# Attention outputs computed channel-major, with normalised probabilities, in a hybrid RWKV-7 and sliding-window attention layer

## The chip, the core and the metric

The kernel runs on one core of a Trainium2 chip. The metric is the time on the device in microseconds (us) of one execution; smaller is better. TensorE (PE, its weight loads PEld) multiplies matrices into the PSUM banks, VectorE (DVE), ScalarE (ACT) and GpSimd (POOL) work elementwise, and SyncE (SP) and ScalarE issue DMA transfers. Each engine runs its instructions in the order in which the program lists them, and waits for the others by semaphores.

## The reference

One decoder layer for 1,024 tokens and 2,048 channels. An RMS norm feeds one input projection (6,528 columns), whose columns go to two groups of heads: RWKV-7 time mixing (16 heads of 64) and sliding-window attention (16 query heads of 64, 2 key/value heads, window 128, blocks of 128 queries). Gated outputs of both are joined, projected and added to the input. The change is in the attention:

```python
logits = einsum('bnqhgd,bnkhd->bnhgqk', qb, kb) * HEAD_DIM ** -0.5   # kb: previous and own block
logits = where(mask, logits + bias, -inf)
m = maximum(max(logits, -1), sink)
e = exp(logits - m)
p = e / (sum(e, -1) + exp(sink - m))
o = einsum('bnhgqk,bnkhd->bnqhgd', p, vb)
return o * silu(g)
```

## The kernel before

The tokens are taken in two halves of 512 (4 blocks of 128). For each half, `hprep` makes the transposed input, and then 8 units follow, one per pair of heads of each kind. A unit has six "z tiles": each is 48 main matmuls of 128x512 into one of two `z` banks (L346 and L347 by turns, then four of L351, for each of four quarters of the contraction). Of a unit's six, three feed the RWKV part (`rwkv_prep`, `rwkv_chain`, `rwkv_post`), one its gate, and two the attention `att` (queries and gate). After both halves the output projection (L786 to L788) runs. Main matmuls take float32 operands split into two float32r parts; the small matmuls of the attention and of RWKV are plain float32.

The order on each engine is made when the program is built. Every step carries a due time (the numbers behind `yield`, set by `at`), in a planner's microseconds: a main matmul counts 0.32, a z tile 15.36, a unit 92.16. Among the instructions that can go, the one with the smallest due time goes first. Matmuls of the z tiles so fill what the small steps leave. `att` counts from the start of its own unit, and `rwkv` too. The attention of a unit is due 99 to 143 after the unit's start, so most of it lies in the next unit, 92.16 later: its output matmuls (due +133) at 40.84 of the next unit, in the third z tile (which starts at 30.72), beside that unit's `rwkv_prep` (due +0.3 to +59). In `rwkv_prep` the chain is: L390 and L391 (matmuls, due +18.5) into `m` banks; L393 to L405 (activations and a scan, L399); L554 and L555 (a sum over heads, in `headsum`); L409 to L427 (VectorE makes Gt and F); L437 (matmuls of Gt and F, due +55 and +59).

Tiles of one name (tag) share a fixed number of buffers: three PSUM banks for `m`, five SBUF buffers of 128x512 for `ta`.

In `att` one unit handles two heads. For each, scores are made (L682 to L690), biased (L695), reduced to a maximum, exponentiated on ScalarE with the row sums (L704), and VectorE takes the reciprocals `sm` of the sums with the sink's part (L705, L706). The unnormalised probabilities of the four blocks are transposed on TensorE (L711) and split by the mask into the part for the own block's keys `pc` (L714) and the previous one's `pv` (L715). The output matmuls (L723 for `pc`, L725 for `pv`) have the probabilities as weights (128x128) and 64 columns of values as the moving side; they give query-major outputs. VectorE multiplies by `sm` (L730, one instruction per head), TensorE transposes the result (L734), and VectorE multiplies with the gate (L736). ScalarE issues the DMA of the result (L737).

Of the kernel before, what the change touches and what calls it, by code (L numbers as in the profile page):

```python
# [14 lines left out]
ALU = mybir.AluOpType  # L15
# [4 lines left out]
P = 128  # L20
# [8 lines left out]
NB = T // P  # L29
# [35 lines left out]
def layer(tc, x, norm_w, w_in, w_out, mu_rwkv, w0, w2, a0, a2, k_k, k_a, r_k, lnx_w, lnx_b,  # L65
# [7 lines left out]
    V, A, G, PE = nc.vector, nc.scalar, nc.gpsimd, nc.tensor  # L73

    def sb(shape, tag, bufs=1, dt=F32):
        return pool.tile(list(shape), dt, name=tag, tag=tag, bufs=bufs)

    HR = (slice(0, 64), slice(64, 128))
    NT = dict(t=4, ta=5, zt=5, wr=4, wh=3, wl=3)

    def tmp(tag="t"):
        return sb([P, T], tag, NT.get(tag, 1))

    def ps(tag, shape=(P, 512)):
        return psum.tile(list(shape), F32, name=tag, tag=tag, bufs={"z": 2, "m": 3, "o": 1, "ch": 1}[tag])
# [6 lines left out]
    def at(t):  # L92
        tc.cur_priority = 100000 + int(t * 1000)
# [24 lines left out]
    ident, causal, mT, ind2 = cs[:, 0:128], cs[:, 128:256], cs[:, 256:384], cs[:, 384:386]  # L118
# [92 lines left out]
    vt = sb([P, NB + 1, P], "vt")  # L211
# [23 lines left out]
    def rsqrt(v, n, tag):  # L235

        y = sb([P, n], tag + "y", 2)
        a = sb([P, n], tag + "a", 2)
        V.tensor_scalar(y[:].bitcast(I32), v.bitcast(I32), -0.5, MAGIC, ALU.mult, ALU.add)
        for _ in range(3):  # L240
            V.tensor_tensor(a[:], y[:], y[:], ALU.mult)
            V.scalar_tensor_tensor(a[:], v, -0.5, a[:], ALU.mult, ALU.mult)
            V.scalar_tensor_tensor(y[:], a[:], 1.5, y[:], ALU.add, ALU.mult)
        return y
# [312 lines left out]
    def silu2(g):  # L557

        tg = tmp("ta")
        A.activation(tg[:], g, AF.Tanh, scale=0.5)  # L560
        s = sb([P, T], "sil", 2)
        V.scalar_tensor_tensor(s[:], tg[:], 1.0, g, ALU.add, ALU.mult)
        return s
# [95 lines left out]
    def att(t0, hf, p, Q, sq, gz):  # L659
        yield t0 + 99  # L660
        sil = silu2(gz[:])
        yield t0 + 103
        pq = ps("m")
        for b in range(NB):
            PE.matmul(pq[:, b * 2:b * 2 + 2], lhsT=sq[:, b * P:(b + 1) * P], rhs=ind2, start=True, stop=True)
        ms = sb([P, 8], "qms", 2)
        V.tensor_scalar(ms[:], pq[:, 0:8], 1.0 / 64, 1e-6, ALU.mult, ALU.add)
        rq = rsqrt(ms[:], 8, "q")
        bia = sb([P, 2, P], "bia")
        nc.sync.dma_start(bia[:], bass.AP(tensor=bd.tensor, offset=bd[p:p + 1, 0:1].offset, ap=[[P - 1, P], [8 * P * P, 2], [1, P]]))  # L670
        yield t0 + 108.5
        pts, sms = [], []
        Ls = [tmp("ta")[:].rearrange("p (b k) -> p b k", b=NB) for _ in range(2)]
        for b2 in range(2):
            yield t0 + 103.5 + 4 * b2
            pls = [ps("m", (P, 2, 256)) for _ in range(2)]
            for b in range(2):
                lb = b2 * 2 + b
                ks = 1 if hf * NB + lb == 0 else 0
                qs, kc = slice(lb * P, (lb + 1) * P), slice((lb + ks) * P, (lb + 2) * P)  # L680
                for i, pl in enumerate(pls):
                    PE.matmul(pl[:, b, ks * P:256], lhsT=Q[:, i, qs], rhs=kh[i][:, kc], start=True, stop=False)  # L682
                    PE.matmul(pl[:, b, ks * P:256], lhsT=Q[:, i, qs], rhs=kl[i][:, kc], start=False, stop=True)
            for pl, L3 in zip(pls, Ls):
                if hf == 0 and b2 == 0:
                    V.memset(L3[:, 0, :], NEG)
                    A.copy(L3[:, 1, :], pl[:, 1, 0:128])
                else:
                    A.copy(L3[:, b2 * 2:b2 * 2 + 2, :], pl[:, :, 0:128])
                V.copy_predicated(L3[:, b2 * 2:b2 * 2 + 2, :], causal_i[:, None, :].to_broadcast([P, 2, P]), pl[:, :, 128:256])  # L690
        for i, L3 in enumerate(Ls):
            hd = p + 8 * i
            yield t0 + 105 + 7 * i
            for b in range(NB):
                V.scalar_tensor_tensor(L3[:, b, :], L3[:, b, :], rq[:, b * 2 + i:b * 2 + i + 1], bia[:, i, :], ALU.mult, ALU.add)  # L695
            mx = sb([P, NB], "mx", 2)
            V.tensor_reduce(mx[:], L3, axis=AX.X, op=ALU.max)
            nm = sb([P, NB], "nm", 2)
            V.tensor_scalar(nm[:], mx[:], snk[:, hd:hd + 1], -1.0, ALU.max, ALU.mult)
            es = sb([P, NB], "es", 2)  # L700
            A.activation(es[:], nm[:], AF.Exp, bias=snk[:, hd:hd + 1])
            sm = sb([P, NB], "sm", 4)
            for b in range(NB):
                A.activation(L3[:, b, :], L3[:, b, :], AF.Exp, bias=nm[:, b:b + 1], accum_out=sm[:, b:b + 1])  # L704
            V.tensor_tensor(sm[:], sm[:], es[:], ALU.add)  # L705
            V.reciprocal(sm[:], sm[:])  # L706
            sms.append(sm)
            yield t0 + 125 + 2 * i
            pt = ps("m", (P, NB, P))
            for b in range(NB):  # L710
                PE.transpose(pt[:, b, :], L3[:, b, :], ident)  # L711
            pc, pv = tmp("ta"), tmp("ta")
            r3 = lambda t: t[:].rearrange("p (b k) -> p b k", b=NB)
            V.tensor_tensor(r3(pc), pt[:], mT[:, None, :].to_broadcast([P, NB, P]), ALU.mult)  # L714
            V.tensor_tensor(r3(pv), pt[:], r3(pc), ALU.subtract)  # L715
            pts.append((r3(pc), r3(pv)))

        yield t0 + 133
        po = ps("m", (P, NB, 2, 64))
        for b in range(NB):  # L720
            blk = hf * NB + b
            for i in range(2):
                PE.matmul(po[:, b, i, :], lhsT=pts[i][0][:, b, :], rhs=vt[:, b + 1, i * 64:(i + 1) * 64], start=b == 0 and i == 0, stop=False, skip_group_check=True)  # L723
                if blk > 0:
                    PE.matmul(po[:, b, i, :], lhsT=pts[i][1][:, b, :], rhs=vt[:, b, i * 64:(i + 1) * 64], start=False, stop=b == NB - 1 and i == 1, skip_group_check=True)  # L725
        ot = tmp("ta")
        o4 = ot[:].rearrange("p (b i v) -> p b i v", b=NB, i=2)
        at(t0 + 125)
        for i in range(2):
            V.tensor_tensor(o4[:, :, i, :], po[:, :, i, :], sms[i][:, :, None].to_broadcast([P, NB, 64]), ALU.mult)  # L730
        yield t0 + 143
        po = ps("m")
        for b in range(NB):
            PE.transpose(po[:, b * P:(b + 1) * P], ot[:, b * P:(b + 1) * P], ident)  # L734
        y = tmp("ta")
        V.scalar_tensor_tensor(y[:], po[:], 0.5, sil[:], ALU.mult, ALU.mult)  # L736
        nc.scalar.dma_start(yd[hf, NP + p], y[:])  # L737
# [146 lines left out]
```

## Time and profile before

| | |
|---|---|
| median of 3 runs | 2084.99 us (2084.62 to 2093.28) |
| profiled execution | 2082.83 us |
| its span, first to last instruction | 2081.0 us |
| mean granted TensorE clock | 0.989 |

The span is the time between the first and the last instruction of the profiled execution; what lies around it, 1.8 us, is not seen in the trace. An engine's busy time says how long it had an instruction in work; TensorE's matmuls are pipelined, so the duration of one (some 400 ns for a main matmul) is longer than the distance to the next (some 235 ns). The distances are what counts on TensorE.

### The profile page before, as it was taken

To read this page: it belongs to the slowest core of one execution; us is meant where nothing else is said; L and a number is where in the kernel's file an instruction comes from. 1 tells how busy PE (TensorE), PEld (TensorE's weight loads), DVE (VectorE), ACT (ScalarE), POOL (GpSimd) and SP (SyncE) were. 2 spreads that over 40 slices of the span, in tenths; PEclk is the share of its full clock that TensorE was granted. 3 is DMA by queue.
4 is the path that set the end of the run, shared out by engine and by line. 5 is a ranking of instruction groups with operands and counts; after the bars stand their busy time and mean duration, and the time that the engine had idled before them with its cause. 6 is when DMAs were issued, how large, how long until landed. Compare 5 with 4: busy or idle time off the path is not lost. (4 is left out here: it accounts for less than half of the span.)

```text
span 2081.0 us, 36561 instructions
## 1 busy us (share of the span) xinstructions
PE 1990.9 (96%) x13216; PEld 1638.3 (79%) x13216; DVE 1158.1 (56%) x2680; ACT 1034.9 (50%) x2563; POOL 862.9 (41%) x740
## 2 busy tenths in 40 slices
PE   7999999999999998998999999999999989999999
PEld 5777778787878786776878787877778778988887
DVE  5647575748475765756565666757575763011001
ACT  5455556465656464735546464555546463223221
POOL 4643444434353433244443534343443433444443
PEclk9999999999999999999999999999999989999999
DMA  7332323332332325123232323232323353555443
GB/s 179 94 85 69 82 72 87 76 81 70 81 86 70 91 60 150 57 77 73 72 83 62 94 57 95 61 92 66 80 72 86 75 166 116 154 156 170 135 137 117
DMA packets 412293, 197.02 MB, mean 95 GB/s; under 512 B 216941, under 2 KB 381136, under 8 KB 412112
## 3 DMA queue, kind: packets, MB, share of 16 engines
q1 hardware_dynamic: 371360, 181.90, 31.9%
q10 hardware_dynamic: 40000, 11.67, 2.3%
q0 software_dynamic: 752, 1.11, 0.5%
q8 instruction: 104, 1.70, 0.3%
q14 instruction: 77, 0.63, 0.1%
HBM read 173.51 MB, written 21.10 MB: 94 GB/s over the span
## 5 line engine op out<-in xcount | busy, mean ns | idle before, releaser
L322 POOL TENSOR_TENSOR wl<-wr,wh 128x512 fp32r<-128x512 f32 x536 | 711.2, 1331 | 1095.3 <-ACT wh L321 497.9
L346 PE MATMUL z<-hh,wh 128*128 128x512 f32 x1632 | 669.2, 410 | 8.7 <-ACT ta L650 6.6
L347 PE MATMUL z<-hl,wh 128*128 128x512 f32 x1632 | 651.1, 399 | 0.6 <-DVE hl L263 0.6
L321 ACT CAST wh<-wr 128x512 fp32r<-128x512 f32 x536 | 329.6, 618 | 465.3 <-PE z L347 158.1
L351 PE MATMUL z<-hh,wl 128*128 128x512 f32 x1632 | 468.8, 402 | 0.3 <-POOL wl L322 0.3
L346 PEld LDWEIGHTS z<-hh,wh 128*128 128x128 f32 x1632 | 309.0, 189 | 77.1 <-ACT ta L650 7.0
L347 PEld LDWEIGHTS z<-hl,wh 128*128 128x128 f32 x1632 | 309.2, 189 | 58.7 <-DVE hl L263 1.2
L351 PEld LDWEIGHTS z<-hh,wl 128*128 128x128 f32 x1632 | 297.7, 189 | 60.4 <-POOL wl L322 1.0
L353 DVE TENSOR_TENSOR z<-z,R 128x512 f32<-128x512 f32 x102 | 70.9, 695 | 137.4 <-PE z L351 134.5
L786 PE MATMUL z<-wh,hh 128*128 128x256 f32 (+1 forms) x352 | 113.1, 322 | 4.1 <-DVE ta L794 4.1
L588 DVE SCALAR_TENSOR_TENSOR svu<-ch,pe,s 64x64 f32<-64x64 f32 x224 | 63.3, 282 | 95.8 <-PE ch L584 91.8
L788 PE MATMUL z<-wh,hl 128*128 128x256 f32 (+1 forms) x352 | 112.3, 319 | 0.0
L787 PE MATMUL z<-wl,hh 128*128 128x256 f32 (+1 forms) x352 | 112.0, 318 | 0.0
L580 ACT ACTIVATE s<-svu,pe 64x64 f32<-64x64 f32 x256 | 88.2, 344 | 39.1 <-DVE svu L588 35.3
L577 PEld LDWEIGHTS o<-svu,F 128*128 128x128 f32 x512 | 78.2, 189 | 16.2 <-DVE svu L588 4.6
L794 DVE TENSOR_TENSOR ta<-z,ta 128x256 f32<-128x256 f32 (+1 forms) x22 | 10.0, 491 | 126.6 <-PE z L788 126.1
L437 PE MATMUL m<-F,Gt 64*128 64x128 f32 x512 | 52.8, 296 | 28.1 <-DVE F L427 14.3
L577 PE MATMUL o<-svu,F 128*128 128x64 f32 x512 | 77.6, 265 | 1.9 <-ACT svu L535 1.3
L437 PEld LDWEIGHTS m<-F,Gt 64*128 64x128 f32 x512 | 42.3, 193 | 44.3 <-issue 26.7
L794 DVE TENSOR_TENSOR ta<-m,ta 128x512 f32<-128x512 f32 x9 | 6.1, 690 | 124.8 <-PE m L788 124.8
L786 PEld LDWEIGHTS z<-wh,hh 128*128 128x128 f32 x352 | 68.0, 193 | 9.0 <-DVE ta L794 3.4
L787 PEld LDWEIGHTS z<-wl,hh 128*128 128x128 f32 x352 | 68.1, 194 | 4.3
(278 smaller groups left out, 3388.9 us busy)
## 6 DMA issues: line engine op xcount, KB each, us to landing
wr<-in_w_in SPq DMA_DIRECT2D x280, 256.0 KB, 2.9
wr<-in_w_in SPq DMA_DIRECT2D x256, 128.0 KB, 2.5
wr<-in_w_out SPq DMA_DIRECT2D x64, 256.0 KB, 3.0
wr<-in_w_out SPq DMA_DIRECT2D x128, 128.0 KB, 2.9
ta<-in_x SPq DMA_DIRECT2D x37, 256.0 KB, 5.2
zt<-yd SPq DMA_DIRECT2D x32, 256.0 KB, 3.3
out<-ta SPq DMA_DIRECT2D x24, 256.0 KB, 3.9
yd<-ta ACTq DMA_DIRECT2D x16, 256.0 KB, 2.0
```

The source lines that it names most:

```text
L321: A.copy(hi[:], raw)
L322: G.tensor_tensor(lo[:], raw, hi[:].bitcast(F32), ALU.subtract)
L346: PE.matmul(z[:], lhsT=wh, rhs=hh[kk][:], start=(kk == 0), stop=False)
L347: PE.matmul(z[:], lhsT=wh, rhs=hl[kk][:], start=False, stop=False)
L351: PE.matmul(z[:], lhsT=lo[:, k * P:(k + 1) * P], rhs=hh[kk][:], start=False, stop=(kk == KT - 1))
L353: V.tensor_tensor(z[:], z[:], R[:], ALU.mult)
L437: PE.matmul(b[:, c, :], lhsT=Gt[hr, c0 + c, :], rhs=F[c0 // 4][hr, i, c, :], start=True, stop=True)
L577: PE.matmul(O[:, c, i, :], lhsT=F[c // 4][:, i, c % 4, :], rhs=svu[:, i, c, :], start=c % 4 == 0 and i == 0, stop=False, skip_group_check= ...
L580: A.activation(s0[hr], svu[hr, i, c, :], AF.Copy, scale=pe[hr, c:c + 1])
L786: PE.matmul(o, lhsT=yh[k][:, ts], rhs=wh, start=k == 0 and tt % n == 0, stop=False, skip_group_check=True)
L787: PE.matmul(o, lhsT=yh[k][:, ts], rhs=wl, start=False, stop=False, skip_group_check=True)
L788: PE.matmul(o, lhsT=yl[k][:, ts], rhs=wh, start=False, stop=k == KT - 1 and tt % n == n - 1, skip_group_check=True)
```

## The change

The reciprocal `sm` of the sums is applied ahead of the transposes: four scalings of 128x128 per head on VectorE (eight per unit). The transposes are due 2 later. The output matmuls have operands swapped: 64 columns of values are the weights, 128 columns of probabilities the moving side, and the outputs come channel-major, one head in each half of the output partitions (`HR`). They are due at +137, not +133. The two multiplications behind them and the transposes of the outputs go, and the gate multiplication reads the outputs' bank directly.

```diff
-        pts, sms = [], []
+        pts = []
...
             V.reciprocal(sm[:], sm[:])
-            sms.append(sm)
-            yield t0 + 125 + 2 * i
+            for b in range(NB):
+                V.tensor_scalar(L3[:, b, :], L3[:, b, :], sm[:, b:b + 1], None, ALU.mult)
+            yield t0 + 127 + 2 * i
             pt = ps("m", (P, NB, P))
             for b in range(NB):
                 PE.transpose(pt[:, b, :], L3[:, b, :], ident)
...
-
-        yield t0 + 133
-        po = ps("m", (P, NB, 2, 64))
+        yield t0 + 137
+        po = ps("m")
         for b in range(NB):
             blk = hf * NB + b
-            for i in range(2):
-                PE.matmul(po[:, b, i, :], lhsT=pts[i][0][:, b, :], rhs=vt[:, b + 1, i * 64:(i + 1) * 64], start=b == 0 and i == 0, stop=False, skip_group_check=True)
+            ts = slice(b * P, (b + 1) * P)
+            for i, hr in enumerate(HR):
+                PE.matmul(po[hr, ts], lhsT=vt[:, b + 1, i * 64:(i + 1) * 64], rhs=pts[i][0][:, b, :], start=b == 0, stop=False, skip_group_check=True)
+            for i, hr in enumerate(HR):
                 if blk > 0:
-                    PE.matmul(po[:, b, i, :], lhsT=pts[i][1][:, b, :], rhs=vt[:, b, i * 64:(i + 1) * 64], start=False, stop=b == NB - 1 and i == 1, skip_group_check=True)
-        ot = tmp("ta")
-        o4 = ot[:].rearrange("p (b i v) -> p b i v", b=NB, i=2)
-        at(t0 + 125)
-        for i in range(2):
-            V.tensor_tensor(o4[:, :, i, :], po[:, :, i, :], sms[i][:, :, None].to_broadcast([P, NB, 64]), ALU.mult)
-        yield t0 + 143
-        po = ps("m")
-        for b in range(NB):
-            PE.transpose(po[:, b * P:(b + 1) * P], ot[:, b * P:(b + 1) * P], ident)
+                    PE.matmul(po[hr, ts], lhsT=vt[:, b, i * 64:(i + 1) * 64], rhs=pts[i][1][:, b, :], start=False, stop=b == NB - 1, skip_group_check=True)
         y = tmp("ta")
         V.scalar_tensor_tensor(y[:], po[:], 0.5, sil[:], ALU.mult, ALU.mult)
```

## Rows read from the trace of the kernel before

**Rows 1.** The page, part 1: busy time, share of the span, instructions.
```profile
PE 1990.9 (96%) x13216; PEld 1638.3 (79%) x13216; DVE 1158.1 (56%) x2680; ACT 1034.9 (50%) x2563; POOL 862.9 (41%) x740
```

**Rows 2.** Windows, sixth to seventh unit: length, busy time (instructions), clock, DMA.
```profile
core 0: us, PE busy (x) PEld busy (x) DVE busy (x) ACT busy (x) POOL busy (x), PEclk, DMA share, GB/s
592.00:667.60 75.60, 73.70 (x568) 60.03 (x569) 43.15 (x120) 44.32 (x122) 28.90 (x25) 1.00 0.32 83
667.60:689.40 21.80, 20.91 (x111) 17.27 (x109) 20.13 (x36) 10.21 (x20) 11.40 (x11) 1.00 0.26 61
```

**Rows 3.** Groups by line: busy us, mean ns | idle before, released by.
```profile
L437 PE MATMUL m<-F,Gt 64*128 64x128 f32 x512 | 52.8, 296 | 28.1 <-DVE F L427 14.3 <-DVE F L441 13.8
L723 PE MATMUL m<-vt,ta 128*128 128x64 f32 x256 | 45.8, 266 | 0.0
L725 PE MATMUL m<-vt,ta 128*128 128x64 f32 x224 | 42.8, 273 | 0.4 <-DVE ta L715 0.4
L730 DVE TENSOR_TENSOR ta<-m,sm 128x256 f32<-128x256 f32 x32 | 11.7, 408 | 7.7 <-PE m L725 7.7
L706 DVE RECIPROCAL sm<-sm 128x4 f32<-128x4 f32 x32 | 5.7, 178 | 1.1
```

**Rows 4.** Timeline of TensorE, output matmuls of the sixth unit: start, us, instruction.
```profile
672.78 0.33 PE L723 MATMUL m<-vt,ta 128*128 128x64 f32 x2
672.92 0.48 PE L390 MATMUL m<-lr,wla 128*128 128x512 f32 x1
...
674.32 0.39 PE L725 MATMUL m<-vt,ta 128*128 128x64 f32 x2
674.54 0.39 PE L723 MATMUL m<-vt,ta 128*128 128x64 f32 x2
...
675.41 0.48 PE L554 MATMUL m<-vh,bonr 128*128 128x512 f32 x1
```

**Rows 5.** Timeline of TensorE, from the output transposes to L437.
```profile
684.72 0.60 PE L734 MATMUL m<-cst,ta 128*128 128x128 f32 x4
685.08 0.48 PE L346 MATMUL z<-hh,wh 128*128 128x512 f32 x1
...
687.71 0.39 PE L347 MATMUL z<-hl,wh 128*128 128x512 f32 x1
688.03 0.49 PE L437 MATMUL m<-F,Gt 64*128 64x128 f32 x2
689.44 1.13 PE L437 MATMUL m<-F,Gt 64*128 64x128 f32 x14 [0.93 <-DVE F L427]
690.50 0.50 PE L346 MATMUL z<-hh,wh 128*128 128x512 f32 x1
```

**Rows 6.** Timeline of VectorE in the same stretch.
```profile
677.30 1.23 DVE L399 TENSOR_TENSOR_SCAN sig<-rmask,sig 128x520 f32<-128x520 bf16 x1
678.45 0.73 DVE L730 TENSOR_TENSOR ta<-m,sm 128x256 f32<-128x256 f32 x2
...
679.77 0.69 DVE L414 TENSOR_TENSOR t<-zt,t 128x512 f32<-128x512 f32 x1
...
688.88 0.42 DVE L427 TENSOR_TENSOR F<-zt,Pc 64x256 f32<-64x256 f32 x1
```

**Rows 7.** Timeline of ScalarE in the same stretch.
```profile
679.12 0.62 ACT L405 ACTIVATE t<-sig 128x512 f32<-128x512 f32 x1
```

**Rows 8.** Timeline of TensorE in the first unit.
```profile
77.46 0.40 PE L390 MATMUL m<-lr,wla 128*128 128x512 f32 x1
...
107.36 1.16 PE L437 MATMUL m<-F,Gt 64*128 64x128 f32 x16
```

**Rows 9.** Timeline of TensorE, second half, first unit's attention beside the second.
```profile
1039.53 0.48 PE L390 MATMUL m<-lr,wla 128*128 128x512 f32 x1
...
1058.08 1.11 PE L734 MATMUL m<-cst,ta 128*128 128x128 f32 x4 [2.42 <-DVE ta L730]
```

**Rows 10.** Timeline of VectorE in the same stretch.
```profile
1041.70 1.24 DVE L399 TENSOR_TENSOR_SCAN sig<-rmask,sig 128x520 f32<-128x520 bf16 x1 [3.90 <-POOL sig L395]
...
1053.15 0.42 DVE L427 TENSOR_TENSOR F<-zt,Pc 64x256 f32<-64x256 f32 x1
```

## The prediction

> **What bounds the kernel now.** I read the page first: TensorE is busy 96% of the span [rows 1], so a saving counts only where TensorE is not waiting for something else. Next I read the timeline of one stretch (the sixth unit's attention beside the seventh's RWKV preparation) engine by engine, then the unit in windows. Of the 97 us between two ends of the RWKV chain, the 75.6 us before the chain's end are TensorE's: 73.7 us busy, VectorE 43.2 us. In the 21.8 us behind it VectorE is busy for 20.1 us, and TensorE ends that stretch waiting [rows 2]. The wait is L437: it starts at 688.03, then stands 0.93 us for the F tiles of L427, which VectorE finishes at 688.88 + 0.42 = 689.30 [rows 5, 6]. The groups by line say that this is no accident: L437 idles 14.3 us on L427 and 13.8 us on L441, about one microsecond each in 13 of 16 units [rows 3]. Those two waits tie TensorE to VectorE once per unit. The removed work (L723, L725, L734) lies just ahead of the first one [rows 4, 5].
>
> **TensorE, per unit.** A float32 matmul stands as two records here: 16 calls, 32 records (28 in the first half's units, whose first block has no previous one) [rows 3]. Before, two records take 674.54 - 674.32 = 0.22 us, so 32 take 3.5 us [rows 4]. After, each record loads 64 columns and streams 128, to one half of the columns of the array. No row shows that shape. Upper bound: the halves don't overlap and a record costs 0.112 as now, 3.6 us. The nearest row that uses half the array, with two row halves by turns and 128 streamed columns, is L437: from 689.44 to 690.50, 14 records, 0.076 each with the way out of the half-array shape [rows 5]; 32 x 0.076 = 2.4 us. I take 2.4, since both are alternating halves of one array. The way in costs 688.03 - 687.71 = 0.32 where a main matmul takes (687.71 - 685.08)/11 = 0.24, so 0.08 [rows 5]; the run is cut in three by L390 and L554 as now [rows 4], 0.25 in all. L734 goes: 685.08 - 684.72 = 0.36, and some 0.08 that the next main matmul needs to start again, 0.44 [rows 5]. TensorE's work falls by 3.5 - 2.4 - 0.25 + 0.44 = 1.3 us per unit; bounds 0.1 (no overlap) and 2.0 (records at half of 0.112).
>
> The Trainium skill, "TensorEngine Tiling", section Performance Considerations, offers exactly this swap (the small moving side made stationary, then two column tiles) for up to 2x; an estimate by it is 32 x 0.056 = 1.8 us, the second bound. "TensorE: Matmul & The Clock Gate", section Part 3, speaks against it: it says that a weight load overlaps a running matmul only if the row group differs, and both halves here share all rows. The trace doesn't bear that out for whole-array matmuls, since loads take 1638.3 us beside 1990.9 us of matmuls in a span of 2081.0 [rows 1]; no row shows it for column halves.
>
> **VectorE, per unit.** Eight scalings of 128x128 are new. Their price is bounded by the reciprocal of 128x4, 0.178 us, and by L730, which has twice the elements, 0.408 us [rows 3]: 1.4 to 3.3 us; I take the middle, 2.2. They follow the sums, some 10 us ahead of the transposes, in the stretch where VectorE has 75.6 - 43.2 = 32 us free [rows 2]. So I cost them at nothing. Behind each wait the row sums of the other head and the chain's L588; without that cover they would cost up to 16 x 2.2 = 35 us. The two L730 go, 0.73 us in the full stretch [rows 6]. That seems a gain, but L414 behind them also reads the output of ScalarE's L405, which ends at 679.12 + 0.62 = 679.74, and L414 starts at 679.77 [rows 6, 7]. So what is late next is L405, behind L401 and L399, and the removal is worth nothing. L736 stays, due earlier but still behind F's operations (due +32 of the next unit). The output's DMA moves earlier on ScalarE's queue, and nobody waits for it before the output projection. The accumulator's bank is now held from the matmuls to L736; before, two tiles held one bank over nearly the same time.
>
> **The moved matmuls.** This is the part that costs. L390 of the next unit is due 18.5 after that unit's start and L437 55 after it. In the first unit, with no attention ahead, they run 107.36 - 77.46 = 29.9 us apart [rows 8]; in the seventh only 688.03 - 672.92 = 15.1, and L390 stands directly behind the first matmul of L723 [rows 4]. I read this as the order of the three banks of "m": the accumulator of the attention outputs is asked for earlier in the program, so L390's bank comes after it. If so, moving the outputs from +133 to +137 takes L390 along. Between the two due times lie 13 main matmuls (four of L351, eight of the next quarter, one more of L351): 13 x 0.235 = 3.05 us, and L390 comes at about 675.97 where it came at 672.92.
>
> How soon can F then be ready? The chain L390, L393, L395, L399, L414, L410, L427 had slack, because L399 (677.30) also stood behind the layer norm on VectorE. The second half's second unit shows the chain without a layer norm ahead: L390 at 1039.53 [rows 9], L399 at 1041.70, the last L427 needed at 1053.15 + 0.42 [rows 10], 14.04 us. So F is ready at 675.97 + 14.04 = 690.0, not at 689.30: 0.7 us later, in spite of the 3.05. From the other side: L399 came 1041.70 - 1039.53 = 2.17 behind L390 there, so 678.14 here, and F was ready 689.30 - 677.30 = 12.0 behind L399 in the seventh unit: 690.1, 0.8 later. I take 0.7. The bounds are nothing (L390 keeps its place) and 3.05 (no slack at all).
>
> TensorE itself now comes to L437 earlier, with only 31 main matmuls between L390 and L437 in place of 44. Whether the saved 1.3 us are worth anything depends on whether the build-time order lets more main matmuls go ahead of L437. It does so only if it thinks F late: in the second half, L734 of the first unit was put where its input seemed ready, and TensorE still waited 2.42 us [rows 9]. So the order expects VectorE 1 to 2.4 us faster than it is. By that the order sees F ready 11.7 to 13.0 us behind L390, and L437's due place comes 31 x 0.235 + 1.4 (L390, L391, L554, L555) + 3.5 = 12.2 us behind it, if it prices the outputs' matmuls as now: it moves L437 by 0 to 3 matmuls, and by up to 9 if it sees their full saving. I take two, 0.47 us.
>
> **Sum.** Per unit with the wait: + 0.70 - 0.47 = + 0.23, times 13: + 3.0 us. The first unit of the second half loses L734's wait: - 2.4 [rows 9]. The last units of each half have no L437 right behind, so their TensorE saving shows: 2 x - 1.3 = - 2.6, of which I take 2. Together - 1.4. The profiled execution took 2082.83 us (span 2081.0 and 1.8 around it), 2.2 below the median of the runs, 2084.99. 2082.83 - 1.4 = 2081.4; I say 2082, no measurable change.
>
> **Rivals.** *The order follows the saving.* L437 moves back by some six to nine main matmuls and the waits of L427 shrink: 13 x (0.7 - 9 x 0.235) = - 18, and - 4.4 from the other units: 2060; with six matmuls 2070. For it: L437 has slack behind it. Against it: the second wait, on L441, follows 6 us behind on VectorE whatever TensorE saves. *TensorE bound throughout*, by the swap's full rate: 16 x (3.5 - 1.8 + 0.44) = 34 us less, 2049. Against it: rows 2, where VectorE fills the stretch. *The other side: F's chain decides.* If L390 moves and L437 keeps its place, each unit is longer by what F is later: 13 x 0.7 to 0.8 = + 9 to + 10, less up to 4 from the other units: 2088 to 2091, and 2093 if column halves don't overlap, since the other units then gain nothing either. If each unit also lets one scaling (0.28) stand ahead of a late L588, 16 x 0.28 = 4.4 us come on top: 2097. It decides from 0.8 us per unit on. If weight loads are not hidden for column halves, each record pays half a load, 1638.3/13216/2 = 0.06 [rows 1], 2.0 us per unit: 2093 + 32 = 2125; I give it 3 in 100. That would be the skill's rule on row groups, above.
>
> **Chances.** As forecast 0.42, range of this case 2073 to 2092; order follows 0.29; TensorE bound 0.07; F's chain or loads 0.22. A measurement of this kernel tells a change from none at about 0.5%, 10 us. Faster 0.36, same 0.42, slower 0.22. The range, 2060 to 2097, holds the first rival and most of the last.
>
> **What would show it.** L390 should stand about 13 main matmuls later in its unit, directly behind the first output matmul, and L427 should end some 0.7 us later against the chain's end. Right behind, L437's wait on L427: near 1 to 2.5 us per unit if I am right; gone if the order followed. Records of the output matmuls should start 0.06 to 0.11 us apart. New waits of L577 or L584 on L588 would mean that the scalings are not hidden. I am wrong if L390 keeps its place (then F comes no later and the saving shows) or if L437's place moves by more than five matmuls.

## The result, and the profile after

The changed kernel takes 2101.39 us (median of 20 runs, 2090.06 to 2117.31), the one before 2088.68 beside it: ratio 1.007, 95% interval 1.0053 to 1.0088. It is slower by 0.7%, outside the forecast range (2060 to 2097). The profiled execution after is the fastest of its runs, 2090.06 us, at a mean granted clock of 0.986.

Page, part 1, and the groups by line after (busy us, mean ns | idle before, released by), against [rows 1, 3]. L724 and L727 are the new output matmuls, L708 the scalings, L715 and L716 the mask operations (L714 and L715 before), L712 the transposes (L711):

```profile
PE 2001.7 (96%) x13152; PEld 1621.2 (78%) x13152; DVE 1201.4 (58%) x2776; ACT 1038.0 (50%) x2563; POOL 857.1 (41%) x740
```

```profile
L437 PE MATMUL m<-F,Gt 64*128 64x128 f32 x512 | 69.7, 299 | 23.0 <-DVE F L427 22.9
L724 PE MATMUL m<-ta,vt 128*64 128x128 f32 x256 | 35.0, 283 | 0.0
L708 DVE TENSOR_SCALAR ta<-ta,sm 128x128 f32<-128x128 f32 x128 | 31.2, 307 | 1.1
L605 DVE TENSOR_TENSOR t<-t,mn 128x512 f32<-128x512 f32 x16 | 24.2, 1511 | 0.1
```

The output matmuls became cheaper, but TensorE is busy for longer. One group of old work grew: L437, 52.8 to 69.7 us for the same 512 records. The timeline of TensorE after, output matmuls and then L437 (in the seventh unit's preparation, as [rows 4, 5]):

```profile
686.69 0.40 PE L346 MATMUL z<-hh,wh 128*128 128x512 f32 x1
686.93 0.39 PE L347 MATMUL z<-hl,wh 128*128 128x512 f32 x1
687.16 0.40 PE L351 MATMUL z<-hh,wl 128*128 128x512 f32 x1
687.49 0.43 PE L724 MATMUL m<-ta,vt 128*64 128x128 f32 x2
687.85 0.50 PE L390 MATMUL m<-lr,wla 128*128 128x512 f32 x1
...
690.40 0.38 PE L724 MATMUL m<-ta,vt 128*64 128x128 f32 x2
690.51 0.27 PE L727 MATMUL m<-ta,vt 128*64 128x128 f32 x1
690.61 0.27 PE L724 MATMUL m<-ta,vt 128*64 128x128 f32 x1
690.62 0.38 PE L727 MATMUL m<-ta,vt 128*64 128x128 f32 x2
...
702.65 1.98 PE L437 MATMUL m<-F,Gt 64*128 64x128 f32 x16 [1.59 <-DVE F L427]
704.56 0.50 PE L347 MATMUL z<-hl,wh 128*128 128x512 f32 x1
...
705.91 1.16 PE L437 MATMUL m<-F,Gt 64*128 64x128 f32 x8
...
709.11 1.13 PE L437 MATMUL m<-F,Gt 64*128 64x128 f32 x8
```

Three things are to be seen. L390 stands directly behind the first output matmul, as before, but now in the 45th place of its z tile and not the 32nd: 13 main matmuls later. L437's wait is 1.59 us where it was 0.93 [rows 5]; its second wait, on L441, is gone. And its records run at 704.56 - 702.65 = 1.91 us for 16, the second group in two pieces of eight; before, 14 took 1.06, after two that took some 0.5 ahead of the wait [rows 5]. The order in which the program lists TensorE's instructions says why. Before (the first matmuls of a unit's L437, second half; the number is the line of the list, and each name ahead of the arrow is the bank of one half):

```
4787 L437 MATMUL m_13271<-F_13207,Gt_13206 128x128
4788 L437 MATMUL m_13279<-F_13207,Gt_13206 128x128
4789 L437 MATMUL m_13271<-F_13207,Gt_13206 128x128
4790 L437 MATMUL m_13279<-F_13207,Gt_13206 128x128
```

and after (the same for another unit of the second half; the first half's units are alike):

```
6185 L437 MATMUL m_17555<-F_17499,Gt_17498 128x128 x3
6186 L437 MATMUL m_17563<-F_17499,Gt_17498 128x128 x3
...
6198 L437 MATMUL m_17591<-F_17500,Gt_17498 128x128 x4
6206 L437 MATMUL m_17599<-F_17500,Gt_17498 128x128 x4
```

A matmul of L437 has 64 rows, one half of the array. By turns a record takes 1.06 / 14 = 0.076 us, in runs of one half 1.91 / 16 = 0.119: two halves are at work at once only by turns.

The timeline of VectorE after, from the end of the RWKV chain (679.40) to F, against [rows 6]:

```profile
678.82 0.58 DVE L588 SCALAR_TENSOR_TENSOR scar<-ch,pe,s 64x64 f32<-64x64 f32 x2 [1.26 <-PE ch L584]
679.94 0.69 DVE L715 TENSOR_TENSOR ta<-m,cst 128x512 f32<-128x512 f32 x1 [0.54 <-PE m L712]
...
681.18 0.68 DVE L716 TENSOR_TENSOR ta<-m,ta 128x512 f32<-128x512 f32 x1
681.78 0.68 DVE L715 TENSOR_TENSOR ta<-m,cst 128x512 f32<-128x512 f32 x1
...
682.50 0.69 DVE L716 TENSOR_TENSOR ta<-m,ta 128x512 f32<-128x512 f32 x1
683.10 1.62 DVE L605 TENSOR_TENSOR t<-t,mn 128x512 f32<-128x512 f32 x1
...
686.82 1.14 DVE L242 SCALAR_TENSOR_TENSOR lna<-ve,lna 128x8 f32<-128x8 f32 x1
688.00 1.22 DVE L243 SCALAR_TENSOR_TENSOR lny<-lna,lny 128x8 f32<-128x8 f32 x1
...
690.87 0.69 DVE L611 TENSOR_TENSOR t<-t,lny 128x512 f32<-128x512 f32 x1
691.48 1.24 DVE L399 TENSOR_TENSOR_SCAN sig<-rmask,sig 128x520 f32<-128x520 bf16 x1
692.63 0.67 DVE L729 SCALAR_TENSOR_TENSOR ta<-m,sil 128x512 f32<-128x512 f32 x1
...
701.30 1.20 DVE L427 TENSOR_TENSOR F<-zt,Pc 64x256 f32<-64x256 f32 x1
...
702.94 0.42 DVE L427 TENSOR_TENSOR F<-zt,Pc 64x256 f32<-64x256 f32 x1
```

Four mask operations stand between the chain's end and the layer norm's L605 (two before), L605 takes 1.62 us, and L399 stands behind the layer norm's last step (L611). L399 starts 691.48 - 679.40 = 12.08 us behind the chain's end (8.88 before, 677.30 [rows 6] against 668.43), and F is ready 703.36 - 679.40 = 23.96 behind it (before: 689.30 - 668.43 = 20.87): 3.1 us later. In the second half it is 23.25 against 21.30, 2.0 us later. L437's wait ends with the first piece of F (701.30 + 1.20 = 702.50), since a run of one half needs no more to begin; 703.36 is the second piece.

And the clock. Windows of the stretch from just ahead of L437's wait in the second half's third unit after (1167.1 to 1176.0; the columns are those of [rows 2]):

```profile
1167.10:1168.70 1.60, 0.10 (x1) 0.00 (x0) 1.54 (x3) 0.57 (x1) 0.00 (x0) 1.00 0.59 135
1168.70:1170.30 1.60, 1.56 (x13) 1.40 (x14) 1.56 (x4) 0.00 (x0) 0.00 (x0) 1.00 0.13 29
1170.30:1173.60 3.30, 3.30 (x13) 2.59 (x10) 3.23 (x8) 0.99 (x2) 0.72 (x1) 0.50 0.21 79
1173.60:1176.00 2.40, 2.40 (x14) 1.78 (x14) 2.34 (x5) 0.24 (x2) 0.57 (x1) 0.98 0.24 54
```

TensorE idles for 1.5 us, works 1.6 us at 2.4 GHz, and then 3.3 us at 1.2 GHz (granted clock 0.50). Of the eleven such waits (1.52 to 1.59 us) in the twelve unit periods of the profiled run, five were followed by such a stretch; none of the 22 waits of 0.9 to 1.1 us of before was. Which waits are followed differs from run to run: over the 20 runs the mean clock goes from 0.986 to 0.969 and the span with it from 2088.3 to 2115.5. Call span x (1 - mean clock) the loss to the clock; a straight line through the 20 runs has 0.68 us of span for each us of loss (correlation 0.94). The median loss is 47.2 us after and 29.2 before (the 17 runs of before that were taken beside e1). 18 x 0.68 = 12.2 us: about the whole difference of the medians (12.7). The run of after with before's median clock, 0.986, took 2090.06, 1.4 us more than before.

The twelve full unit periods of a profiled run (the second to the seventh unit of each half, between ends of the RWKV chain) show the rest. "Periods" is their length in sum, "idle" TensorE's idle times over 0.1 us in them. L437, outputs and main (the main matmuls) are the time from such an instruction's start to the next one's on TensorE, without the idle times, summed. Then comes the loss to the clock in the periods; the last two columns are medians over the runs. e1 to e17 are the experiments below:

```
              periods   idle   L437  outputs   main   loss in periods | median us   loss
before         1198.2   31.7   37.3    37.2    868.7        1.7       |  2088.7     29.2
after          1210.1   30.3   51.2    27.5    877.8        8.5       |  2101.4     47.2
e1             1187.0   32.4   36.2    27.5    870.1        0.0       |  2069.3     26.9
e2             1199.9   26.8   49.4    27.5    872.1        0.0       |  2092.6     34.5
e3             1221.8   48.1   38.5    25.9    888.0       23.9       |  2103.3     50.4
e11            1214.1   34.1   47.4    27.5    885.6       12.0       |  2103.2     39.9
e10            1200.9   34.7   33.6    27.6    879.6       12.0       |  2089.5     42.8
e15            1198.7   32.2   27.5    27.5    868.6        0.0       |  2086.4     25.0
e17            1190.1   19.5   32.6    27.5    867.5        0.0       |  2079.0     31.2
```

(e15 and e17 have 17 us of added transposes in the periods besides.) Outputs fell by 9.6 us, L437 rose by 13.9, idling stayed as it was.

### The profile page after: what moved, and what is told of

It is laid out like the page before. It is cut to its first block, busy times and chain, and to the rows that moved or that the text cites. A ratio compares the mean times of both kernels' runs of the same rounds, so it can differ in the third digit from the quotient of the medians.

```text
span 2088.3 us, 36503 instructions
## 1 busy us (share of the span) xinstructions
PE 2001.7 (96%) x13152; PEld 1621.2 (78%) x13152; DVE 1201.4 (58%) x2776; ACT 1038.0 (50%) x2563; POOL 857.1 (41%) x740
## 4 chain that ended last, share of the span: by engine, by line
PE 39%; DVE 9%; ACT 3%; issue 2%; DMA 2%; POOL 1%; SPq 0%; ACTq 0%; POOLq 0%; DVEq 0%
PE z L346 6%; PE z L351 6%; PE z L347 6%; PE m L437 2%; PE z L779 2%; PE z L781 2%; PE z L780 2%; PE m L779 2%; PE m L780 2%; PE m L781 2%; DVE t L410 1%; PE o L577 1%; PE o L779 1%; PE o L780 1%; PE o L781 1%
## 5 line engine op out<-in xcount | busy, mean ns | idle before, releaser
L322 POOL TENSOR_TENSOR wl<-wr,wh 128x512 fp32r<-128x512 f32 x536 | 705.8, 1321 | 1127.6 <-ACT wh L321 503.6
L346 PE MATMUL z<-hh,wh 128*128 128x512 f32 x1632 | 670.2, 411 | 10.9 <-ACT ta L650 6.6
L321 ACT CAST wh<-wr 128x512 fp32r<-128x512 f32 x536 | 329.9, 618 | 454.0 <-PE z L347 145.6
L351 PE MATMUL z<-hh,wl 128*128 128x512 f32 x1632 | 475.0, 404 | 0.3 <-POOL wl L322 0.3
L346 PEld LDWEIGHTS z<-hh,wh 128*128 128x128 f32 x1632 | 310.9, 191 | 78.9 <-ACT ta L650 7.0
L437 PEld LDWEIGHTS m<-F,Gt 64*128 64x128 f32 x512 | 58.8, 197 | 43.5 <-issue 17.4
L437 PE MATMUL m<-F,Gt 64*128 64x128 f32 x512 | 69.7, 299 | 23.0 <-DVE F L427 22.9
L514 DVE COPY Erb<-m 64x256 f32<-64x256 f32 x64 | 26.9, 421 | 80.6 <-ACT k L513 79.9
```

What stands on the lines that cost most here:

```text
L321: A.copy(hi[:], raw)
L322: G.tensor_tensor(lo[:], raw, hi[:].bitcast(F32), ALU.subtract)
L346: PE.matmul(z[:], lhsT=wh, rhs=hh[kk][:], start=(kk == 0), stop=False)
L351: PE.matmul(z[:], lhsT=lo[:, k * P:(k + 1) * P], rhs=hh[kk][:], start=False, stop=(kk == KT - 1))
L437: PE.matmul(b[:, c, :], lhsT=Gt[hr, c0 + c, :], rhs=F[c0 // 4][hr, i, c, :], start=True, stop=True)
```

## The experiments

**The due times apart.** Theories for the first eight runs: A, the transposes' later due time puts the mask operations into the layer norm and delays F; B, the outputs' due time carries L390 and its chain along; C, the scalings cost time on VectorE.

e1: the changed computation at the old due times.

```diff
-            yield t0 + 127 + 2 * i
+            yield t0 + 125 + 2 * i
...
-        yield t0 + 137
+        yield t0 + 133
```

> The changed kernel with the old due times (transposes +125 and +127, output matmuls +133), everything else as changed. Theory A (the transposes' later due time puts the two mask operations of both heads into the next unit's layer norm on VectorE): from the chain's end to L399 some 8.9 us again instead of 12.1, F ready about 21 us behind the chain's end instead of 24, and about 2060 to 2075 us. Theory B (the output matmuls' later due time, with L390 behind them, is what costs): the same. Theory C (the scalings cost, whatever the due times): no faster than the changed kernel, 2090 to 2105.

2069.32 us, ratio 0.991 (0.9893 to 0.9925): faster than both kernels. L399 is back at 8.89 us behind the chain's end, F at 20.5; L437's halves go by turns, its waits are 0.9, 0.4 and 0.6 us, and no stretch of the periods is at the lower clock. The computation gains 19 us; the due times cost 32.

e2: the changed kernel with the old due time of the transposes alone (+125); e3: with the old one of the outputs alone (+133).

> The changed kernel with the transposes at the old +125 and +127 and the output matmuls at +137. Theory A: the layer norm is as fast as in the kernel before, L399 waits at most for L390's chain, some 10.6 us behind the chain's end, F ready at about 22.5: between, 2070 to 2085. Theory B: the cost stays in full, L399 at about 12 and the time near the changed kernel's, 2090 to 2105.

> The changed kernel with the transposes at +127 and +129 and the output matmuls at the old +133. Theory A: the layer norm stays late, L399 about 12 us behind the chain's end, time near the changed kernel's, 2085 to 2105. Theory B: most of the cost is gone, L399 near 9, 2060 to 2080.

e2: 2092.57, ratio 1.0018 (1.0001 to 1.0036); e3: 2103.31, 1.0062 (1.0048 to 1.0076). Each move alone costs some 1.1 to 1.5% against e1, and by different means. In e2 L390 moves, F is ready at 23.35 us behind the chain's end in the first half (21.47 in the second), and L437 comes in runs: 49.4 against 36.2 us in the periods, which is their whole difference (12.9). The time is the one that B gave, but L399 starts at 10.2, not at B's 12. In e3 L390 stays and L437 goes by turns, but F is ready at 23.6:

```profile
L437 PE MATMUL m<-F,Gt 64*128 64x128 f32 x512 | 52.3, 312 | 43.1 <-DVE F L427 41.6 <-DVE F L441 1.5
```

The time is in A's range, but not by A's way: L399 starts at 9.0, not at 12, ahead of the late layer norm's end, and it is L409 and L414 that come behind it (L414 starts at 13.7; 11.35 in e1). Idle time rises by 15.6 us against e1 and the loss to the clock by 23.9. The changed kernel has the split halves of e2, waits of 1.5 us, and a loss to the clock close to e3's; the two costs don't add up.

e4: the old computation with the new due times (+127 and +129, +137, +129, +147).

> The kernel before with its computation unchanged and only the due times moved as in the change: transposes +127 and +129, output matmuls +137, the multiplications +129, the output transposes +147. Theories A and B (due times cost): slower than before by 1 to 3 us per unit, 2100 to 2125, more than the changed kernel since nothing is saved on TensorE. Theory C (the scalings cost): as before, within 0.5%.

2137.14, ratio 1.023 (1.0212 to 1.0247), above the range of A and B: L734 waits 37.0 us for L730, and the median loss is 61.9. The order costs the old computation more than the new one.

**The computation.** e5: e1 without the scalings.

```diff
-            for b in range(NB):
-                V.tensor_scalar(L3[:, b, :], L3[:, b, :], sm[:, b:b + 1], None, ALU.mult)
```

> The changed kernel with the old due times and without the eight scalings per unit: the division by the sums is left out, so the attention outputs are not normalised; all else as in the run with the old due times (2069 us). Theory C0 (the scalings lie under other work, as the prediction had it): 2064 to 2071 us. Theory C (they cost what they take, 128 x 0.307 us on VectorE): up to 39 us less, 2030 to 2050. Between them: they delay L588 and so the chain, some 10 us less.

2074.12, ratio 0.9937 (0.992 to 0.9955), no faster than e1 (2069.32): the scalings are hidden; C falls.

e6: e1 with the outputs of one half ahead of those of the other (the loop over the heads outside that over the blocks).

> The changed kernel with the old due times, and the output matmuls in another order: all of one half of the output partitions, then all of the other, in place of the two halves by turns. If the 0.055 us between records come from two column halves at work at the same time, the records go back to about 0.11 and each unit pays some 1.5 us more on TensorE; the time lies between 2069 and 2090, near 2080 when what is added shows in part. If a record of 64 weight columns simply takes 0.055 us, nothing changes, 2069.

2086.84, ratio 0.9994 (0.9983 to 1.0005): 17.5 us, 1.1 per unit, are lost. Outputs take 39.9 us in the periods against 27.5: column halves do work at once, by turns alone.

**Moving further.** e7: old due time of the transposes, outputs at +139, so that their bank is asked for after L390's. e8: transposes at +121, outputs at +129.

> The changed kernel with the transposes at the old +125 and +127 and the output matmuls at +139, so that the program asks for their bank after the banks of the next unit's L390 (which it does from 138.24 on). Theory B as the order of the banks: though the outputs come later than in the changed kernel, L390 no longer stands behind them, L399 is back at about 8.9 us behind the chain's end, and the time is 2060 to 2080. If it is the late output matmuls themselves that cost, 2085 to 2105.

> The changed kernel with the transposes at +121 and +123 and the output matmuls at +129, 4 earlier than in the run with the old due times. Theories A and B carry on: the mask operations leave the layer norm and L390 comes earlier, so F is ready up to 1.3 us sooner per unit; 2050 to 2069 us. Against it, scaled probabilities that are not ready (a wait of L712 on L708), or a wait of L437 on its banks: 2069 to 2085.

e7: 2100.23, ratio 1.0055 (1.0039 to 1.0071); L390 jumps ahead, before the chain's end, which confirms the order of the banks, though the time is not the one it was to give (2060 to 2080). e8: 2095.09, 1.0032 (1.0017 to 1.0047), above both of its ranges. Against e1, F comes 0.9 to 2 us earlier in e8's first half (0.9 earlier to 0.3 later in the second), and up to 1.3 later in e7. Neither gains, since another wait comes up ahead of it; in e7:

```profile
L555 PE MATMUL m<-vl,bonr 128*128 128x512 f32 x34 | 16.1, 473 | 24.6 <-POOL vl L552 24.4
```

In e8 it is 33.2 us; their losses to the clock are 44.1 and 46.1.

**L437: halves, waits, clock.** Here theory H says that the split halves are the main loss and that TensorE sets the unit's length; W, that VectorE's chain before and behind L437 sets it. e11: e1 with the halves in runs.

```diff
-                yield t0 + 55 + c0
+                yield t0 + 55 + c0 + 0.1 * i
```

> The faster variant (changed computation at the old due times, 2069 us) with one change: the second row half of L437 is due 0.1 later than the first, so that four calls of one half stand ahead of four of the other; the places among the main matmuls stay as they were to within two. Theory H: two row halves do work at once only by turns; 512 records at 0.13 in place of 0.09 us cost about 1.1 us per unit, 16 to 18 us in all: 2084 to 2088. Theory W: TensorE waits for F at this place anyway, the split costs less than a third of that: 2068 to 2074.

2103.18, ratio 1.0058 (1.0038 to 1.0079), 34 us above e1, twice what H priced. L437 takes 11.2 us more in the periods, as H has it; 12.0 more are lost to the clock, and L346 now waits for the weights' cast (L321), 14.0 us, which neither foresaw. L437's wait is 0.9 us here, as in e1, and yet four of eleven such waits were followed by a slow stretch (in e1 none of eleven). Windows of one, from the wait on:

```profile
599.10:600.00 0.90, 0.04 (x1) 0.00 (x0) 0.87 (x2) 0.00 (x0) 0.53 (x1) 1.00 0.56 127
600.00:602.40 2.40, 2.35 (x15) 1.89 (x16) 2.34 (x6) 0.00 (x0) 0.00 (x0) 1.00 0.50 116
602.40:605.80 3.40, 3.40 (x11) 2.69 (x11) 3.31 (x8) 1.75 (x4) 0.00 (x0) 0.50 0.00 0
```

e9: the changed kernel with L437 due 3 later; e10 and e12: e1 with L437 due 2 and 3 later (`yield t0 + 57 + c0`, or 58).

> The changed kernel with one change: L437 due 3 later (+58 and +62 for +55 and +59). In the built order its two row halves stand by turns again in most units, some five main matmuls further back; in the changed kernel they stand in runs of three or four calls of one half. Over twelve unit periods of each trace the time from one start on TensorE to the next, without waits, is 51.2 us at L437 in the changed kernel and 37.3 before. Theory H: this split is the main loss, 1.1 us per unit, and TensorE sets the length of a unit. Then L437 comes down to some 40 us per twelve periods, its wait of 17 us shrinks as main matmuls fill it, and the time falls from 2101 to 2065 to 2085. Theory W: the wait for VectorE's F tiles sets the unit, and the split only takes time in which TensorE would wait. Then what is saved at L437 comes back as a wait further on (L577, L584, L555), and the time stays between 2095 and 2115.

> The faster variant with L437 due 2 later (+57 and +61). In the built order it stands seven and five main matmuls further back (1.6 and 1.2 us), with its halves by turns. Theory H: TensorE's work sets the length of a unit and the waits at L437 (22.5 us in twelve periods, 1.9 per unit) are idle time that these matmuls fill: the time falls by 15 to 30 us, to 2039 to 2055. Theory W: the chain on VectorE behind L437 (L438 to L441, the solve, the state's chain) sets the unit: what L437 is later comes back as later waits, 2062 to 2085.

> The faster variant with L437 due 3 later (+58 and +62): ten and eight main matmuls further back (2.4 and 1.9 us), halves by turns. Theory H: the waits at L437 are gone; the time is that of L437 two later within 5 us, or lower, 2035 to 2055. Theory W: each matmul further back makes the chain behind it later; slower than with two later, 2065 to 2095.

e9: 2120.40, 1.0152 (1.0132 to 1.0172); e10: 2089.48, 1.0005 (0.9992 to 1.0017); e12: 2106.32, 1.0086 (1.0067 to 1.0106). All slower than where they started, against H, and above W's ranges too. (In e9's first half L437 stands only one main matmul further back, in the second the five expected.) With 3, new waits of L522 for L441 come up (18.6 us in e12's periods, 7.7 in e9's), which is W. In e10 none does: idle time is 34.7 us against e1's 32.4, L437 even shorter; but the waits of 0.9, 0.4 and 0.6 us have become one of 1.67 us per unit, on L441. Windows behind it in e10, and TensorE's timeline there:

```profile
697.10:698.80 1.70, 0.03 (x1) 0.06 (x1) 1.64 (x5) 0.83 (x2) 1.45 (x2) 1.00 0.52 117
698.80:700.40 1.60, 1.34 (x15) 1.18 (x16) 1.60 (x3) 0.40 (x1) 0.47 (x1) 0.95 0.00 0
700.40:703.60 3.20, 3.20 (x11) 2.40 (x9) 3.09 (x8) 1.61 (x4) 1.28 (x1) 0.50 0.35 102
```

```profile
701.38 0.63 PE L346 MATMUL z<-hh,wh 128*128 128x512 f32 x1
701.81 0.63 PE L347 MATMUL z<-hl,wh 128*128 128x512 f32 x1
...
703.82 0.39 PE L346 MATMUL z<-hh,wh 128*128 128x512 f32 x1
704.05 0.39 PE L347 MATMUL z<-hl,wh 128*128 128x512 f32 x1
```

Main matmuls start 0.43 us apart there, 0.23 behind it. So a third theory, K: the clock after a long wait is the cost.

e13: e10 with one small unused matmul ahead of L437's second group, which reads what the first L441 wrote; e14: the changed kernel with one ahead of the first group, reading the first piece of F.

> The variant with old due times and L437 two later (2089.5 us), with one small matmul (64 rows, 64x128, its result is not used) put directly ahead of the second group of L437. It reads a tile that the first of the two L441 has written, some 0.7 us before the second one, for which L437 stands. No other instruction of TensorE changes its place, and the sum of the waits stays: the single wait of 1.67 us in each unit is cut into two of about 1.0 and 0.6 us. Theory K (the clock): what makes that variant 20 us slower than the one with the old place of L437 is that its single long wait is followed by a stretch at 1.2 GHz in most units; the waits and the work are the same. Then the low stretches in the units go (23.8 us in twelve periods there, 0 with the old place), the mean granted clock rises from 0.980 to 0.985 or more, and the time falls to 2070 to 2080. Theory W (the chain on VectorE behind L437 sets the unit): the clock makes no difference to the time, 2086 to 2094.

> The changed kernel with one small matmul (64x64, its result is not used) ahead of the first group of L437, reading the first piece of F, which VectorE has finished some 0.4 us before the piece that L437 stands for. L437 keeps its place; its first group comes by turns of the halves in most units, since it is planned one step later. Theory K: the wait of 1.59 us is cut into some 1.15 and 0.4, the low stretches (17 us in twelve periods of the profiled run, more in the others) go or get fewer, mean clock from 0.978 to 0.983 or more, and with some 0.5 us per unit less at L437 the time falls from 2101 to 2075 to 2090. Theory W: only what L437 itself saves can show, and that is given back to the chain: 2093 to 2103.

e13: 2082.20, ratio 0.9969 (0.9956 to 0.9983); e14: 2099.33, 1.0056 (1.0039 to 1.0073). e13 lies between the two ranges, e14 in W's, but neither decides, since the slow stretches that were to go did not. The waits were split unevenly (1.58 and 0.4 us in e13, 1.0 to 1.3 and 0.46 in e14). In e13's periods 12.0 us are lost to the clock, as in e10; they are 3.9 us shorter, with 2.9 us less idling, and the 4.9 us less at L437 (28.7 against 33.6) stand against 5.1 for the added matmul. In e14's periods 15.4 us are lost, more than the 8.5 of the changed kernel, and L437 takes 52.2 us although its first group mostly goes by turns: nine slow stretches lie there.

e15: e10 with twelve unused transposes ahead of L437's second group, written to its bank; e17: the same, written to the free `o` bank.

```diff
+                if c0 == 4 and i == 0:
+                    at(t0 + 60.9)
+                    dm = ps("o")
+                    for c in range(12):
+                        PE.transpose(dm[:, c % 4 * P:c % 4 * P + P], cs[:, 0:P], ident)
+                    at(t0 + 61)
```

> The variant with old due times and L437 two later (2089.5 us), with twelve transposes of 128x128 from a constant (some 0.11 us each, 1.3 us in all; their results are not used) directly ahead of the second group of L437, where TensorE waits 1.67 us in each unit. They wait for nothing, and no other matmul changes its place: TensorE does more work, and is only not idle in that time. Theory K (the clock): a long wait is followed by a stretch at 1.2 GHz, and that stretch costs the time. Then the stretches in the units go (23.8 us in twelve periods there), the mean granted clock rises from 0.980 to 0.985 or more, and the time falls to 2068 to 2078, though work was added. Theory W (the chain on VectorE behind L437 sets the unit): the end of the wait is set by VectorE as before, 2087 to 2094. If the transposes take longer than the wait: above 2094.

> As the run before it (old due times, L437 two later, twelve unused transposes of 128x128 directly ahead of the second group of L437), but the transposes write to the o bank, which is free there. In the run before, they wrote to the bank for which L437 itself waits, so they stood behind the wait, added 17 us of work in twelve periods, and the time was nevertheless 2086.4 against 2089.5, with no low stretch in the units. Here they run inside the wait. Theory K: 1.3 us of the 1.67 us are filled, no work comes on top, the low stretches stay away, and the time is that without loss to the clock, 2043.7 + 27 of span: 2068 to 2076. Theory W: the end of the wait is VectorE's, the time stays at 2086 to 2092 whatever the clock does.

e15: 2086.39, ratio 0.9983 (0.9974 to 0.9993). The transposes waited for the bank, so the waits of 1.67 us stayed and 17.2 us of work came on top in the periods; no stretch at the lower clock followed, and the time fell by 3. e17: 2079.04, 0.9946 (0.993 to 0.9963). The timeline of TensorE (here L439 are the transposes, L443 is L437, L447 is L441) shows them inside the wait:

```profile
694.65 1.47 PE L439 MATMUL o<-cst 128*128 128x128 f32 x12
696.48 0.46 PE L443 MATMUL m<-F,Gt 64*128 64x128 f32 x2 [0.36 <-DVE F L447]
697.20 1.13 PE L443 MATMUL m<-F,Gt 64*128 64x128 f32 x14 [0.26 <-DVE F L447]
698.25 0.50 PE L351 MATMUL z<-hh,wl 128*128 128x512 f32 x1
```

The window behind it in e17, to be held against 700.40:703.60 of e10:

```profile
698.30:701.50 3.20, 3.20 (x15) 2.63 (x15) 3.09 (x7) 3.12 (x8) 1.29 (x1) 1.00 0.38 108
```

VectorE's chain and every main matmul are where they were in e10; TensorE does more, and the kernel is 10.4 us faster, with main matmuls 12.1 us shorter in the periods. That is K, though 3 us short of its range. W, in which the chain's end sets the time whatever the clock does, falls for e10. K holds for this wait; e11 shows that a wait need not be long to be followed by a slow stretch. e1 stays the fastest of all.

## Why the prediction was wrong

**TensorE's work: right.** Outputs were to cost 3.5 - 2.4 - 0.25 = 0.85 us less per unit; they cost 9.6 / 12 = 0.80 less. Records start 0.055 us apart (690.51, 690.61, 690.62), the bound that was not taken. The way in costs 687.49 - 687.16 = 0.33 where a main matmul takes 0.23, and two more such ways in follow. The Trainium skill, "TensorEngine Tiling (Array Packing)", section Theoretical Speedup, gives up to 2x for a dimension of 64 or less; inside a run the trace agrees (0.11 to 0.055). The rule of the Trainium skill, "TensorE: Matmul & The Clock Gate", Part 3, on weight loads of one row group, which would have spoken against it, is not borne out by that spacing. L734 was worth 0.40 us, forecast 0.44. Two small slips in its sums change nothing: the upper bound of the saving is 3.5 - 1.8 - 0.25 + 0.44 = 1.9, not 2.0, and the middle of 1.4 and 3.3 (the scalings) is 2.35, not 2.2.

**VectorE's scalings: right.** They take 0.31 us each, and e5 shows them hidden. One reading beside them was wrong: the gate multiplication (now L729) does not stand behind F's operations but at 692.63, between L399 and L409, where the two L730 stood; so the full stretch lost nothing and gained nothing. **The gain of the whole computation** is 19 us in e1, 1.2 per unit, as the TensorE step had it (1.3).

**The moved matmuls: the first step that failed.** L390 moved by the 13 main matmuls forecast, tied by the order of the banks (e7). But "F is ready at 675.97 + 14.04 = 690.0, ... 0.7 us later" did not hold: F came 3.1 us later in the first half and 2.0 in the second. The step followed one of the two moved steps only. The transposes are due 2 later as well; their mask operations slid behind the chain's end, into the layer norm, behind which L399 now stands. Of L399's 3.2 us, 1.3 are that order (L605 starts 683.10 - 679.40 = 3.70 us behind the chain's end, where it was 670.82 - 668.43 = 2.39); 0.9 are L605, which takes 1.62 us for 0.69; and 1.0 are the layer norm's small steps behind it, two of which take 1.14 and 1.22 us (1.27 and 0.54 before; last section). e3, with L390 in its old place, shows that the transposes alone make F as late, by L409 and L414. Nor was 0.7 right for the outputs alone: in e2 F is 2.5 us later in the first half and 0.2 in the second.

**The wait in the sum: the second step that failed.** L437's place moved back by 9 main matmuls in the first half and 5 in the second (two were taken, nine the bound; more than five was named as a sign of being wrong). Its second wait went, and idle time did not grow (31.7 to 30.3 us in twelve periods). That the forecast wait, + 0.23 us per unit, is near this is luck: F was 3.1 us late, not 0.7, and L437's place 2.1 us back, not 0.47, and the two errors nearly cancel. What failed in "+ 0.70 - 0.47 = + 0.23" is that a wait was priced at its length and L437 at its old duration. Two prices were missing. One is that of halves in runs: 1.2 us per unit (13.9 / 12; in e2, without a slow stretch in its periods, 12.1 / 12 = 1.0; e11 shows it by itself), which took the saving of the outputs away. The other is the clock: one wait of 1.5 us brings in many runs a stretch of some 3 us at half speed. With before's mean clock the forecast would have been 8 us off (2090 against 2082), within the range; the clock adds the other 11, as far as one run and the straight line through 20 tell it.

**The rivals.** "F's chain decides" (2088 to 2097) named the direction, by a sum of waits that did not grow. "The order follows the saving" gave a time near e1's (2069), where no due time is moved, but its way is not e1's: there L437 keeps its place, its waits are those of before (22.5 against 21.8 us in twelve periods), and TensorE's saving shows all the same, as in "TensorE bound throughout" with 1.2 us per unit and not 2.1.

**What stays open.** What decides whether a wait is followed by the slow stretch. It is not the length of the wait alone: 0.9 us was in four of eleven in e11, where L437 runs half after half, and in none of eleven in e1; 1.59 us was once in six first-half units of the changed kernel, and never in the profiled run of e2 (0 of 6; other runs of e2 had a mean clock down to 0.977); 1.67 us was in seven of eleven in e10, and never in e15, where dense small matmuls followed it. The changed kernel with its own wait filled wasn't tried. That the clock makes up the 11 us in its median rests on its 20 runs and on e10 against e17, not on an intervention in it.

## What to carry to other kernels

Change a computation and its place in the order separately: here the first gained 0.9% and the second lost 1.5%. When a step is moved later, follow every instruction it issues to the engine on which it lands, and look at how the instructions of its neighbours interleave, not only at when they start. On an engine that is the bound, several short waits can be cheaper than one long one of about the same sum (e1 against e10), though short ones are not safe either (e11): look at the granted clock in the windows behind a wait, and compare the mean clock of many runs.

## What was not expected of the hardware

The slow stretch starts after the wait has ended, not in it: 1.6 us after in the windows shown (1170.30 after a wait that ended at 1168.7), 1.1 to 2.4 us after in the twelve cases of the changed kernel and e10. It lasts about 3.3 us. A main matmul costs 0.43 us in it and 0.23 outside. Filling the wait with useless transposes made a kernel faster (2089.5 to 2079.0).

VectorE's L605, the same 128x512 subtraction, took 1.62 to 1.64 us in 14 of 16 units where it had taken 0.69 in all before. In the unit shown it starts at 683.10 beside a GpSimd operation that runs from 682.89 for 1.29 us; before, it started at 670.82, when GpSimd was free (its operations there began at 668.76 and 671.32):

```profile
682.89 1.29 POOL L322 TENSOR_TENSOR wl<-wr,wh 128x512 fp32r<-128x512 f32 x1 [2.44 <-PE z L351]
686.65 1.29 POOL L322 TENSOR_TENSOR wl<-wr,wh 128x512 fp32r<-128x512 f32 x1 [2.47 <-ACT wh L321]
687.90 1.29 POOL L552 TENSOR_TENSOR vl<-t,vh 128x512 fp32r<-128x512 f32 x1
```

```profile
670.82 0.69 DVE L605 TENSOR_TENSOR t<-t,mn 128x512 f32<-128x512 f32 x1
```

The small steps of the layer norm behind it, 0.17 us each while GpSimd is free, show the same: L242 ends at 686.82 + 1.14 = 687.96, with GpSimd's L322 (687.94), and L243 at 689.22, with L552 (689.19). No run changed GpSimd's work by itself, but the traces of all 18 kernels agree: L605 took 1.62 to 1.64 us all 69 times that it started while a GpSimd instruction was at work, and 0.68 to 0.69 all 219 times that it did not. L608, which reads one input, started so 186 times and took 0.69 each time. The Trainium skill, "GPSIMD Engine Reference", section Specifications, says that GpSimd shares its SBUF interfaces with VectorE, in contention with VectorE's instructions that read two SBUF inputs; L605, L242 and L243 read two, and these rows agree.
